# A 64-row expert block's high and low parts stacked on 128 partitions, with its spreads spaced out over two pairs of PSUM banks

## The chip, the cores and the metric

The kernel runs on one core of one Trainium2 chip. The metric is the device time of one execution in microseconds; three runs of the kernel before have a median of 2049.76 us (2049.07 to 2051.22).

## What is computed

The reference is a long chain for 512 tokens of 1024 features: a first transformer block (FFN, two attentions, FFN), a second one with a convolution and an mLSTM, and last a hierarchical mixture of experts. Only this last part is touched. Every token goes to two of 32 experts, each with 512 inner features; in short:

```python
def hierarchical_moe(h, rg_w, rg_b, re_w, re_b, w_gate, w_up, w_down):
    ...
    def expert_block(args):
        xb, e = args
        a = xb @ w_gate[e]
        u = xb @ w_up[e]
        return (jax.nn.silu(a) * u) @ w_down[e]

    ys = lax.map(expert_block, (xs, block_expert)).reshape(n_slots, D)
    ys = ys * slot_gate[:, None].astype(ys.dtype)
    out = jnp.zeros((T, D), ys.dtype).at[slot_tok].add(ys)
```

## The kernel before

The tokens, sorted by expert, are cut into 32 blocks (`SLOTS`), each of which uses one expert's weights. 27 blocks have 64 rows and are called narrow here; five have 128 rows and are called wide: numbers 6, 11, 16, 21 and 26 (`WIDE_AT`, line 47). A block's weights are six loads of 1 MB: four for gate and up, two for down. The loads go through a ring of 13 buffers (`RINGS`, line 48); `e_done` tells the ring that a part has been used, and `e_advance` issues the next load on SyncE's queue, which waits there until the buffer is free.

`moe_blocks` (line 1790) runs over the blocks in a software pipeline. Iteration i (line 1806) does four things on TensorE:

- the gate/up products of block i+1 (`e_gu`): eight chunks c of 128 features, for each a gate and an up product. For a narrow block the stationary operand has 64 columns, and gate and up fill the two halves of one `mm` bank, as two column tiles of the array that run side by side. A wide block takes two `mm` banks and the whole array. Every fp32 product is two records in the trace;
- the turn of block i (`e_turn`): four transposes of the activated rows `eh` into a `tp` bank, which ScalarE copies to `hT`;
- four spreads of block i-1, one for each tile of 128 tokens (`spread`): the block's results are multiplied with a 0/1 matrix `pick` that has a one where a row belongs to a token, into two banks (`po` for the first 512 features, `tp` for the last), and VectorE adds both banks into `x` (`spread_add`);
- the down products of block i (`e_down`): four chunks c, for each two halves of 512 features, into `sc`. For a narrow block these two halves are again the two halves of one bank's partitions: features 0 to 511 on partitions 0 to 63, features 512 to 1023 on 64 to 127.

After that `keep` makes `pick` (VectorE) and splits the results into a high part, rounded to fp32r by ScalarE, and a low part, the rest, by VectorE's subtraction. Both parts of a narrow block stand in one tile `y` of 128 partitions, high in columns 0 to 511 and low in columns 512 to 1023. The product with `pick` runs in fp32r, once with the high part and once with the low, so that the sum is exact enough. A narrow block's spread has four such products: for each part, one with the upper 64 partitions into `po` and one with the lower 64 into `tp`. A wide block's has four too, of 128 partitions each.

The order on TensorE is the order in the code. `e_gu` calls a hook behind each chunk: behind chunk 1 it makes the turn, and behind chunks 3, 5 and 7 one spread each. The fourth spread is left for the loop at line 1822, which runs after `e_gu` and `e_act` and ahead of `e_down`. In iteration 31, which has no gate/up products, all four spreads stand in that loop.

PSUM has eight banks: three `mm`, two `sc`, two `tp` and one `po` (lines 337 to 347). Each is taken in rotation, and a product that takes one waits until its last use has been read.

Of the kernel before, what the change touches and what calls it, by code (L numbers as in the profile page):

```python
# [8 lines left out]
F32 = mybir.dt.float32  # L9
F32R = mybir.dt.float32r  # L10
I32 = mybir.dt.int32
BF16 = mybir.dt.bfloat16
AF = mybir.ActivationFunctionType
# [303 lines left out]
class Kern:  # L317
# [1416 lines left out]
        self.nc.scalar.activation(t[:, 0:4 * m], p[:, 0:4 * m], AF.Copy)  # L1734
        return t

    def e_down(self, i, h, part=None):

        if part is None:
            part = lambda j: self.e_parts[i, 4 + j]  # L1740
        if i is not None and self.wide(i):
            m, ps = 128, (self.sc(), self.sc())
        else:
            p = self.sc()
            m, ps = 64, (p[0:64], p[64:128])
        for c in range(4):
            for f in range(2):
                o = (c % 2) * 1024 + f * 512
                self.nc.tensor.matmul(ps[f], h[:, c * m:(c + 1) * m], part(c // 2)[:, o:o + 512],
                                      start=(c == 0), stop=(c == 3))  # L1750
            if i is not None and c % 2:
                self.e_done(i, 4 + c // 2)
        return (ps[0], ps[1]) if m == 128 else (p,)

    def yt(self, dt=F32):
# [3 lines left out]
    def keep(self, ps, tok):  # L1759
        nc = self.nc  # L1760
        s = self.et("pick", F32R)
        nc.vector.tensor_scalar(s, self.e_iota, tok, None, op0=ALU.is_equal)
        parts = []
        for p in ps:
            y = self.yt(F32R)
            self.split_act(p, y[:, 0:512], y[:, 512:1024])
            parts.append(y)
        return s, parts

    def spread_to(self, kept, t, banks, first=True, last=True):  # L1770

        s, parts = kept
        n = len(parts)
        for i in range(2):
            for f in range(2):
                a = slice(0, 128) if n == 2 else slice(64 * f, 64 * f + 64)
                self.nc.tensor.matmul(banks[f], s[a, t * 128:(t + 1) * 128], parts[f % n][a, 512 * i:512 * i + 512],
                                      start=first and i == 0, stop=last and i == 1)

    def spread_add(self, t, banks):  # L1780
        for f in range(2):
# [1 line left out]
            self.nc.vector.tensor_add(o, o, banks[f].rearrange("p (c d) -> p c d", c=4))  # L1783

    def spread(self, kept, t):
        banks = self.po(), self.tp()
        self.spread_to(kept, t, banks)
        self.spread_add(t, banks)

    def moe_blocks(self):  # L1790
        nc, tc = self.nc, self.tc
        self.e_advance()
        self.e_iota = self.xpool.tile([128, 512], F32, name="e_iota")
        nc.gpsimd.dma_start(self.e_iota, self.I["c_main"][:, 512:1024])
        gr = self.xpool.tile([128, D], F32, name="gains")
        self.rows_in(ROW_FN, D, gr)
        self.g3 = gr.rearrange("p (c d) -> p c d", c=KC)
        rows = lambda i: (self.block_rows(self.first_row(self.ex[i]), 128 if self.wide(i) else 64)
                          if i < SLOTS else None)
        fac = lambda i: [self.fac[:, j, self.ex[i]:self.ex[i] + 1] for j in range(2)]  # L1800
        x = self.block_rows(self.row1, 64)
        self.by_block()
        xn = rows(2)
        h = self.e_act(self.first, fac(0))
        kept = hT = None
        for i in range(SLOTS):
            todo = [lambda t=t, k=kept: self.spread(k, t) for t in range(4)] if kept else []

            def hook(c):
                nonlocal hT  # L1810
                if c == 1:
                    hT = self.e_turn(h)
                elif c % 2 and todo:
                    todo.pop(0)()
            if i + 1 < SLOTS:
                ps = self.e_gu(i + 1, x, hook)
                x, xn = xn, rows(i + 3)
                hn = self.e_act(ps, fac(i + 1))
            else:
                hook(1)  # L1820
                hn = None
            while todo:
                todo.pop(0)()
            ps = self.e_down(i, hT)
            kept = self.keep(ps, self.tok[:, self.ex[i]:self.ex[i] + 1])
            h = hn
        self.final(kept)


        more = nc.values_load(self.wl[0:1, 2 * PLACES:2 * PLACES + 1], min_val=0, max_val=PLACES - SLOTS)  # L1830
        with tc.For_i(0, more, 1) as it:
            e = nc.sync.value_load(self.wl[0:1, ds(it + SLOTS, 1)], min_val=0, max_val=NE - 1)
            x = self.block_rows(self.first_row(it + SLOTS), 64)
            ix = self.xpool.tile([128, 1], F32, name="m_tok", tag="ix", bufs=1)
            fx = self.xpool.tile([128, 2], F32, name="m_fac", tag="fx", bufs=1)
            nc.vector.tensor_copy(ix, self.tok[:, ds(it + SLOTS, 1)])
            for j in range(2):
                nc.vector.tensor_copy(fx[:, j:j + 1], self.fac[:, j, ds(it + SLOTS, 1)])
            parts = []
            for j in range(6):  # L1840
                t = self.e_raw("raw2")
                nc.sync.dma_start(t, self.I["we"][ds(e, 1), j].rearrange("a p f -> (a p) f"))
                parts.append(t)
            p = self.mm()
            ps = p[0:64], p[64:128]
            for c in range(KC):
                s = slice((c % 4) * 512, (c % 4 + 1) * 512)
                for k in range(2):
                    nc.tensor.matmul(ps[k], x[:, c, 0:64], parts[2 * (c // 4) + k][:, s], start=(c == 0), stop=(c == KC - 1))
            h = self.e_act(ps, [fx[:, j:j + 1] for j in range(2)])  # L1850
            kept = self.keep(self.e_down(None, self.e_turn(h), lambda j: parts[4 + j]), ix)
            self.final(kept)
# [65 lines left out]
```

## Time and profile before

| what | us |
|---|---|
| median of three runs | 2049.76 |
| profiled execution | 2049.38 |
| its span | 2047.5 |
| TensorE busy in the span | 1904.2 |
| VectorE busy | 1067.7 |
| ScalarE busy | 620.7 |
| all 32 blocks, first gate/up products to the end | 577.7 |

The span is the time from the first to the last instruction; the execution's own time is 1.9 us longer. Busy times are sums over an engine's instructions; matmuls overlap, so a busy TensorE is not one at its peak. The first gate/up products start at 1469.8 us. All times below are counted from the start of the span. In a timeline a row may stand for several equal instructions (x8), with the start of the first and the time to the end of the last; what stands in brackets is the engine's idle time ahead of it and who ended it. "128*64" is the part of the array in rows and columns that a product uses.

### The profile page before, as it was taken

The page shows a single profiled execution, that of the slowest core. Times are in us where ns is not written, and L with a number is a line of the kernel's source. Part 1 is how long each engine was busy: PE and PEld are TensorE (multiplying, and loading weights), DVE is VectorE, ACT ScalarE, POOL GpSimd, SP SyncE. Part 2 cuts the span into 40 slices and gives each one's busy share as a digit, 9 for nine tenths or more (in the row PEclk, how much of TensorE's full clock was granted, in tenths as well). Part 3 has the DMA queues.
Part 4 walks back from the last instruction along what each step waited for, and adds up shares of the span by engine and source line. Part 5 has one row for each costly group of instructions (what it writes and reads, how often), then busy time and mean ns, then how long its engine had stood idle before and what let it go on. Part 6 is the DMA issues. An engine that isn't in the chain of part 4 may idle for free.

```text
span 2047.5 us, 22693 instructions
## 1 busy us (share of the span) xinstructions
PE 1904.2 (93%) x8588; PEld 1299.9 (63%) x8588; DVE 1067.7 (52%) x1628; ACT 620.7 (30%) x979; POOL 382.2 (19%) x293
## 2 busy tenths in 40 slices
PE   7999999999999999999999878689499999999995
PEld 5888888887777788888888756567233333333331
DVE  6543344425578555443445789985534444444344
ACT  4322223325565343221324234442321111111112
POOL 2000000125554430000002456524100000000001
PEclk9999999999999999999999989799799999999997
DMA  5233222322222122222222211112799999899981
GB/s 174 83 139 144 85 101 103 123 77 80 87 68 82 62 103 98 88 103 103 84 101 103 73 60 41 42 42 86 294 373 421 419 376 391 334 370 360 369 318 42
DMA packets 52443, 337.89 MB, mean 165 GB/s; under 512 B 5868, under 2 KB 8724, under 8 KB 13804
## 3 DMA queue, kind: packets, MB, share of 16 engines
q1 hardware_dynamic: 48972, 326.13, 41.9%
q0 software_dynamic: 3072, 9.24, 1.5%
q8 instruction: 69, 1.13, 0.2%
q10 hardware_dynamic: 288, 1.05, 0.1%
q14 instruction: 42, 0.34, 0.0%
HBM read 332.18 MB, written 8.16 MB: 166 GB/s over the span
## 4 chain that ended last, share of the span: by engine, by line
PE 81%; DVE 12%; DMA 3%; issue 2%; ACT 1%; POOL 1%; SPq 0%; POOLq 0%; DVEq 0%; ACTq 0%
PE mm L302 64%; PE sc L302 8%; PE po L302 6%; DVE conv L302 4%; PE tp L302 3%; DVE qk L302 2%; DVE x L302 1%; DVE score L302 1%; DMA x_rows<-x 1%; DMA eraw<-in_we_dram 1%; DVE att_s L302 1%; DVE rs_t L302 0%; DMA x<-in_xT_dram 0%; DVE rs_y L302 0%; DMA raw<-in_wd_dram 0%
## 5 line engine op out<-in xcount | busy, mean ns | idle before, releaser
L302 PE MATMUL mm<-nhi,whi 128*128 128x512 f32 x1120 | 446.9, 399 | 13.2 <-ACT whi L356 9.4
L302 PE MATMUL mm<-nlo,whi 128*128 128x512 f32 x1120 | 439.2, 392 | 1.2 <-DVE nlo L302 1.2
L302 PE MATMUL mm<-nhi,wlo 128*128 128x512 f32 x1120 | 438.6, 392 | 0.7 <-DVE wlo L302 0.7
L356 ACT ACTIVATE whi<-raw 128x1024 fp32r<-128x1024 f32 x220 | 231.1, 1053 | 306.8 <-PE mm L302 118.2
L302 DVE TENSOR_TENSOR wlo<-raw,whi 128x1024 fp32r<-128x1024 f32 x155 | 198.1, 1279 | 209.8 <-ACT whi L356 209.8
L302 PE MATMUL mm<-eraw,xb 128*64 128x512 f32 (+1 forms) x992 | 274.0, 603 | 0.0
L302 PEld LDWEIGHTS mm<-nhi,whi 128*128 128x128 f32 x1120 | 211.8, 189 | 62.6 <-ACT whi L356 9.4
L302 PEld LDWEIGHTS mm<-nlo,whi 128*128 128x128 f32 x1120 | 211.7, 189 | 46.7 <-DVE nlo L302 4.1
L302 PEld LDWEIGHTS mm<-nhi,wlo 128*128 128x128 f32 x1120 | 211.5, 189 | 46.6 <-DVE wlo L302 1.7
L302 DVE TENSOR_TENSOR x<-x,po 128x512 f32<-128x512 f32 x124 | 85.2, 687 | 219.9 <-PE tp L302 183.6
L302 POOL TENSOR_TENSOR wlo<-raw,whi 128x1024 fp32r<-128x1024 f32 x65 | 163.8, 2525 | 151.2 <-ACT whi L356 140.1
L302 PEld LDWEIGHTS mm<-eraw,xb 128*64 128x64 f32 (+1 forms) x992 | 81.2, 145 | 133.2 <-issue 125.6
L302 PE MATMUL mm<-hhi,whi 128*128 128x512 f32 x352 | 136.9, 389 | 0.0
L302 PE MATMUL mm<-hlo,whi 128*128 128x512 f32 x352 | 136.9, 389 | 0.0
L302 PE MATMUL mm<-hhi,wlo 128*128 128x512 f32 x352 | 136.9, 389 | 0.0
L302 PE MATMUL sc<-eraw,hT 128*64 128x512 f32 (+1 forms) x512 | 136.8, 609 | 0.0
L302 PE MATMUL po<-y,pick 64*128 64x512 f32 (+1 forms) x248 | 94.5, 447 | 25.1 <-DVE x L302 24.5
L302 POOL TENSOR_TENSOR acc<-sq,sq 128x512 f32<-128x512 f32 x6 | 8.7, 1457 | 580.2 <-ACT sq L455 580.2
L302 PEld LDWEIGHTS po<-y,pick 64*128 64x128 f32 (+1 forms) x248 | 38.4, 186 | 112.8 <-DVE x L302 79.3
L302 POOL TENSOR_SCALAR rs_v<-fss 128x1 f32<-128x1 f32 x3 | 0.6, 190 | 542.4 <-ACT eraw L1866 542.2
L302 PEld LDWEIGHTS sc<-eraw,hT 128*64 128x64 f32 (+1 forms) x512 | 44.1, 147 | 77.2 <-issue 75.3
L302 PE MATMUL tp<-y,pick 64*128 64x512 f32 (+1 forms) x248 | 92.5, 439 | 0.0
(447 smaller groups left out, 2566.8 us busy)
## 6 DMA issues: line engine op xcount, KB each, us to landing
eraw<-in_we_dram SPq DMA_DIRECT2D x192, 1024.0 KB, 7.8
raw<-in_wd_dram SPq DMA_DIRECT2D x109, 1024.0 KB, 4.8
bias_rows<-bias_by_distance SPq DMA_DIRECT2D x4, 960.0 KB
bias<-bias_rows POOLq DMA_DIRECT2D x12, 256.0 KB, 3.1
x_rows<-x SPq DMA_DIRECT2D x4, 512.0 KB, 18.4
x<-in_xT_dram SPq DMA_DIRECT2D x3, 512.0 KB, 8.3
raw<-in_wd_dram SPq DMA_DIRECT2D x2, 512.0 KB, 9.0
out_dram<-eraw SPq DMA_DIRECT2D x2, 512.0 KB
```

Of the source, the lines that this page charges most:

```text
L302: return f(*a, **k)
L356: self.nc.scalar.activation(hi, raw, AF.Copy)
```

## The change

- `keep`: a narrow block's two halves are laid out the other way. For the first 512 features the high part stands on partitions 0 to 63 of `y`'s columns 0 to 511 and the low part on partitions 64 to 127 of the same columns; for the other 512 features, in columns 512 to 1023, the high part stands on 64 to 127 and the low part on 0 to 63. It takes two copies on ScalarE and two subtractions on VectorE of 64 partitions each, in place of one each of 128.
- `spread_to`: a narrow block's spread is two products of 128 partitions, one for each bank, in place of four of 64 partitions. `pick` has the same tokens on both halves of its partitions, so that a product adds high and low part itself. A wide block's four products stay; those for `po` now come ahead of those for `tp`.
- `spread`: tiles 1 and 3 take an `mm` bank in place of `po`.
- `moe_blocks` and `e_down`: the turn comes behind chunk 0 of the gate/up products, the spreads of tiles 0 to 2 behind chunks 3, 5 and 7 as before, and that of tile 3 behind chunk 0 of the down products, by a hook that `e_down` calls.

```diff
-    def e_down(self, i, h, part=None):
+    def e_down(self, i, h, part=None, hook=None):
...
             if i is not None and c % 2:
                 self.e_done(i, 4 + c // 2)
+            if hook:
+                hook(c)
         return (ps[0], ps[1]) if m == 128 else (p,)
...
         parts = []
-        for p in ps:
+        if len(ps) == 1:
+
             y = self.yt(F32R)
-            self.split_act(p, y[:, 0:512], y[:, 512:1024])
+            for f in range(2):
+                a, b, c = slice(64 * f, 64 * f + 64), slice(64 - 64 * f, 128 - 64 * f), slice(512 * f, 512 * f + 512)
+                nc.scalar.activation(y[a, c], ps[0][a], AF.Copy)
+                nc.vector.tensor_sub(y[b, c], ps[0][a], y[a, c].bitcast(F32))
             parts.append(y)
+        else:
+            for p in ps:
+                y = self.yt(F32R)
+                self.split_act(p, y[:, 0:512], y[:, 512:1024])
+                parts.append(y)
         return s, parts
...
         s, parts = kept
-        n = len(parts)
-        for i in range(2):
-            for f in range(2):
-                a = slice(0, 128) if n == 2 else slice(64 * f, 64 * f + 64)
-                self.nc.tensor.matmul(banks[f], s[a, t * 128:(t + 1) * 128], parts[f % n][a, 512 * i:512 * i + 512],
-                                      start=first and i == 0, stop=last and i == 1)
+        w = s[:, t * 128:(t + 1) * 128]
+        for f in range(2):
+            y = parts[f:f + 1] if len(parts) == 2 else parts
+            r = [y[0][:, 0:512], y[0][:, 512:1024]] if len(parts) == 2 else [y[0][:, 512 * f:512 * f + 512]]
+            for i, a in enumerate(r):
+                self.nc.tensor.matmul(banks[f], w, a, start=first and i == 0, stop=last and i == len(r) - 1)
...
     def spread(self, kept, t):
-        banks = self.po(), self.tp()
+        banks = self.mm() if t % 2 else self.po(), self.tp()
...
             def hook(c):
                 nonlocal hT
-                if c == 1:
+                if c == 0:
                     hT = self.e_turn(h)
-                elif c % 2 and todo:
+                elif c % 2 and c > 1 and todo:
                     todo.pop(0)()
...
             else:
-                hook(1)
+                hook(0)
                 hn = None
+                while todo:
+                    todo.pop(0)()
+            ps = self.e_down(i, hT, hook=lambda c: c % 2 == 0 and todo and todo.pop(0)())
             while todo:
                 todo.pop(0)()
-            ps = self.e_down(i, hT)
```

On TensorE, the end of iteration 2, whose three blocks are narrow, before: spread 2 (`po` 10848), spread 3 (`po` 10871), and the down products (`sc`).

```order
L302 MATMUL mm_10800<-eraw_10638,xb_10661 64x512
L302 MATMUL mm_10800<-eraw_10648,xb_10661 64x512
L302 MATMUL po_10848<-y_10797,pick_10795 128x512
L302 MATMUL tp_10849<-y_10797,pick_10795 128x512
L302 MATMUL po_10848<-y_10797,pick_10795 128x512
L302 MATMUL tp_10849<-y_10797,pick_10795 128x512
L302 MATMUL po_10871<-y_10797,pick_10795 128x512
L302 MATMUL tp_10872<-y_10797,pick_10795 128x512
L302 MATMUL po_10871<-y_10797,pick_10795 128x512
L302 MATMUL tp_10872<-y_10797,pick_10795 128x512
L302 MATMUL sc_10879<-eraw_10650,hT_10806 64x512 x4
L302 MATMUL sc_10879<-eraw_10672,hT_10806 64x512 x4
```

The same place now:

```order
L302 MATMUL mm_10796<-eraw_10638,xb_10661 64x512
L302 MATMUL mm_10796<-eraw_10648,xb_10661 64x512
L302 MATMUL po_10840<-y_10791,pick_10789 128x512
L302 MATMUL tp_10841<-y_10791,pick_10789 128x512
L302 MATMUL sc_10861<-eraw_10650,hT_10800 64x512 x2
L302 MATMUL mm_10864<-y_10791,pick_10789 128x512
L302 MATMUL tp_10865<-y_10791,pick_10789 128x512
L302 MATMUL sc_10861<-eraw_10650,hT_10800 64x512 x2
L302 MATMUL sc_10861<-eraw_10672,hT_10800 64x512 x4
```

Each spread has two products in place of four, and spread 3 has moved between the first chunk of the down products and the second, into an `mm` bank.

On ScalarE, what follows the down products of iteration 1, before, with the semaphores that are waited for: the copy that makes `y`, the copy of the turn, and the next block's rows (`xb`).

```order
L362 ACTIVATE y_10797<-sc_10765 128x512 [waits PE_49]
L1734 ACTIVATE hT_10806<-tp_10805 128x256 [waits DVE_49,PE_49]
L1691 TENSOR_LOAD work_list_10383
L1691 ISA x2
L1696 ISA
L1696 ACTIVATE xb_10865<-xs 128x8x64 [waits PE_49,Activation_49]
```

The same place now:

```order
L1771 ACTIVATE y_10791<-sc_10753 64x512 [waits PE_49]
L1771 ACTIVATE y_10791<-sc_10753 64x512 [waits DVE_49]
L1734 ACTIVATE hT_10800<-tp_10799 128x256 [waits PE_49]
L1691 TENSOR_LOAD work_list_10383
L1691 ISA x2
L1696 ISA
L1696 ACTIVATE xb_10855<-xs 128x8x64 [waits PE_49,Activation_49]
```

There are two copies of half the height, and the second waits for VectorE, whose first subtraction reads the same bank; the turn's copy stands behind it.

## Rows read from the trace of the kernel before

**Rows 1.** The page, its first line.

```profile
span 2047.5 us, 22693 instructions
```

**Rows 2.** Windows: length, busy time of each engine, clock, DMA share, GB/s.

```profile
1501.40:1650.00 148.60, 141.83 (x620) 49.66 (x617) 64.07 (x101) 22.85 (x38) 0.00 (x0) 1.00 1.01 421
1650.00:1983.00 333.00, 319.16 (x1307) 116.08 (x1305) 134.78 (x213) 48.14 (x81) 0.00 (x0) 1.00 0.94 363
```

**Rows 3.** Waits of TensorE, 1501.4 to 2022: us in total, times, longest.

```profile
PE po L302 <- DVE x L302: 24.5, 33, 0.8
```

**Rows 4.** Timeline of iteration 13, TensorE, ScalarE, VectorE: start, us, work.

```profile
1704.31 1.89 PE L302 MATMUL mm<-eraw,xb 128*64 128x512 f32 x8
...
1704.52 0.60 ACT L362 ACTIVATE y<-sc 128x512 fp32r<-128x512 f32 x1 [5.02 <-PE sc L302]
...
1705.15 0.69 DVE L302 TENSOR_TENSOR y<-sc,y 128x512 fp32r<-128x512 f32 x1 [2.41 <-ACT y L362]
...
1708.38 0.49 PE L302 MATMUL po<-y,pick 64*128 64x512 f32 x1
...
1709.04 1.94 PE L302 MATMUL mm<-eraw,xb 128*64 128x512 f32 x8
...
1710.91 0.49 PE L302 MATMUL po<-y,pick 64*128 64x512 f32 x1
...
1713.44 0.50 PE L302 MATMUL po<-y,pick 64*128 64x512 f32 x1
...
1714.73 0.68 ACT L1724 ACTIVATE eg<-mm,fac 64x512 f32<-64x512 f32 x1
...
1714.95 0.49 PE L302 MATMUL po<-y,pick 64*128 64x512 f32 x1 [0.78 <-DVE x L302]
...
1715.61 3.65 PE L302 MATMUL sc<-eraw,hT 128*64 128x512 f32 x16
...
1719.10 1.89 PE L302 MATMUL mm<-eraw,xb 128*64 128x512 f32 x8
```

**Rows 5.** Timeline of TensorE, iteration 17: spreads 2 and 3 of wide block 16.

```profile
1784.57 0.50 PE L302 MATMUL po<-y,pick 128*128 128x512 f32 x1
...
1786.31 0.50 PE L302 MATMUL po<-y,pick 128*128 128x512 f32 x1 [0.55 <-DVE x L302]
...
1787.45 1.08 PE L302 MATMUL sc<-eraw,hT 128*64 128x512 f32 x4
```

**Rows 6.** Timeline of TensorE in the mLSTM: fp32 products (`qk`), then fp32r ones.

```profile
1321.19 0.60 PE L302 MATMUL po<-qk,qk 128*128 128x256 f32 x2
...
1321.86 0.39 PE L302 MATMUL mm<-nlo,whi 128*128 128x512 f32 x1
1322.09 0.40 PE L302 MATMUL mm<-nhi,wlo 128*128 128x512 f32 x1
```

**Rows 7.** Timeline of TensorE, iteration 15: gate/up products of wide block 16.

```profile
1742.30 3.70 PE L302 MATMUL mm<-eraw,xb 128*128 128x512 f32 x8
1745.93 0.50 PE L302 MATMUL po<-y,pick 64*128 64x512 f32 x1
...
1746.59 0.70 PE L302 MATMUL mm<-eraw,xb 128*128 128x512 f32 x1
```

**Rows 8.** Timeline of TensorE: first turn, block 6's first products, last down products.

```profile
1492.42 0.46 PE L302 MATMUL tp<-cmain,eh 64*128 64x64 f32 x4
...
1560.75 1.55 PE L302 MATMUL mm<-eraw,xb 128*128 128x512 f32 x3
...
2015.68 6.21 PE L302 MATMUL sc<-eraw,hT 128*64 128x512 f32 x16
```

**Rows 9.** Tile `eraw`, the 36th load (block 6): issue, time to landing.

```profile
L1670 SPq DMA_DIRECT2D eraw<-in_we_dram x1: 333/333/333, 1536.7 to 1536.7; - x1
...
DMA to landing us min/median/max: 19.8/19.8/19.8
```

**Rows 10.** Timeline of weight loads among dense fp32r products.

```profile
897.26 0.19 PEld L302 LDWEIGHTS mm<-nlo,whi 128*128 128x128 f32 x1
```

## The prediction

> **What bounds the kernel now.** I first read the page for the span, 2047.5 us [rows 1], and then the windows over the expert blocks, where the change lies. From 1501 to 1983 us TensorE is busy for 141.8 of 148.6 us and then for 319.2 of 333 us, its clock granted in full [rows 2]. The loads run at 421 GB/s in the first stretch and at 363 GB/s in the second: there the queues are fed as buffers come free, and not the reverse. The waits of TensorE's products in this stage name one releaser that counts, the adds into `x` on VectorE: 24.5 us in 33 waits [rows 3]; no product waits for a load. The timeline of one iteration shows where: spreads 0, 1 and 2 stand alone between gate/up products, but spread 3 follows spread 2 directly and stands idle for 0.78 us, because there is one `po` bank and VectorE has to add it first [rows 4]. So TensorE's row of instructions is the path, and what leaves it comes off the end, as long as the loads keep up.
>
> **What a spread costs, two ways.** In [rows 4] a narrow spread takes 0.66 us from its first product to the next gate/up product (1708.38 to 1709.04). Its four products are two pairs of 64-row tiles; po and tp start together, so a pair costs one stream. The stacked form has two products on all 128 rows, one after the other: again two streams. The nearest row for it is a wide block's spread: four 128-row products in 1.14 us (1786.31 to 1787.45) [rows 5], 0.23 us each by the step of such products in [rows 6] plus 0.22 for entering and leaving; two would take 0.68. Between narrow products I therefore put the stacking at nothing, though it halves the instructions. Its bounds there are 0.2 us less (two streams of 0.23 and no change-over) and 0.19 us more (a weight load that shows, below).
>
> A change-over has a price of its own. Sixteen down records take 3.49 us [rows 4], 0.43 for each pair once the change-over in front is taken off; eight gate/up records between two spreads take 1.87 us (1709.04 to 1710.91), 0.15 more than four times 0.43. Beside wide gate/up products (128 rows by 128 columns, one record at a time) today's 64-row pairs are another array shape: eight records and a spread take 4.29 us (1742.30 to 1746.59), of which 3.44 are records at 0.43 [rows 7]. The stacked spread has the shape of its neighbours there. What such a neighbour costs can be seen where an fp32 product goes over to an fp32r one in another bank, both 128 by 128: from the first of two 256-column records to the second fp32r product it is 0.67 us [rows 6]; two times 0.21 and one 0.23 make 0.65, so next to nothing is lost. A stacked spread among wide products should cost 0.46 us and the cycle 3.90: 0.39 less.
>
> **The sum over iterations 1 to 30**, which have both gate/up products and spreads (wide blocks are 6, 11, 16, 21 and 26):
> - All three blocks narrow, 15 iterations. Now 2.17 us from spread 2 to the down products (1713.44 to 1715.61) [rows 4]. After: spread 2, 0.66, and spread 3 behind the first chunk of the down products, 0.66 and one more change-over, 0.15. 2.17 - 1.47 = 0.70; times 15: 10.5.
> - Wide gate/up products, 5 iterations. The 0.70; 0.39 each for spreads 0 and 1; about 0.20 for spread 2, which saves the way in only, since narrow down products follow. 1.68 times 5: 8.4.
> - Wide down products, 5 iterations. The 0.70; spread 3 among wide down products costs 0.46 and not 0.81, 0.35 less; spread 2's way out, 0.15. 1.20 times 5: 6.0.
> - Spreads of a wide block, 5 iterations. Their products stay as they are. Now 2.88 us from spread 2 to the down products (1784.57 to 1787.45) [rows 5]; after, 1.14 and 1.14 + 0.15: 0.45 less, times 5: 2.3.
>
> Together 27.2 us. At its new place the wait is covered: spread 3 takes a `mm` bank and the tp of spread 1, both added long before, some 1.6 us after spread 2 started.
>
> **Smaller terms.** The turn moves from behind chunk 1 to behind chunk 0. In iteration 0 it waits for block 0's `eh` until 1492.42 [rows 8], so chunk 1 now comes after that wait: 0.9 us lost, once. Keeping a narrow block becomes a chain of four half-height pieces (ScalarE, VectorE, ScalarE, VectorE; the order shows ScalarE's second one waiting for VectorE). Half the height is not half the time: 0.68 us for `eg` with 64x512 on ScalarE beside 0.60 for `y` with 128x512 [rows 4]. So the chain is 2 x (0.60 + 0.69) plus gaps, 2.7 us, where it was 1.3. It starts 0.2 us into the gate/up products and spread 0 comes 4.07 us into them [rows 4], so 1.2 us are left over; behind ScalarE's second wait stand hT's copy, needed only at the down products, and `xb` of a later block. In the last iteration the spreads follow each other directly; three waits of 0.78 us fall away, since two pairs of banks let TensorE run ahead, and the chain's 1.3 us come in: 1.0 us gained. After the last block the chain lies open: its second ScalarE piece with the gaps, while VectorE waits, is about 0.75 us. The last down products run at half clock now (6.21 us where 3.65 is usual) [rows 4, 8], behind the sparse spreads before them. These stay about as sparse, so I leave that; if the clock held, 2.6 us more would go.
>
> Sum: 27.2 - 0.9 + 1.0 - 0.75 = 26.6 us. From the profiled execution, 2049.38 us, that gives 2022.8; it lies 0.4 us below the median of the runs shown, which I neglect.
>
> **Do the loads keep up?** A block is 6.29 MB; at 421 GB/s that is 14.94 us, and a narrow iteration will take 14.1. The stock is thinnest at the start. The load for block 6 that is issued at 1536.7 lands 19.8 us later [rows 9], at 1556.5, for products that start at 1560.75 [rows 8]: 4.2 us in hand. Four iterations will have gained 2.8 by then and iteration 0 lost 0.9, so 2.3 remain, and then a wide block takes longer than its loads. Later, five iterations with one wide block need 31.5 MB in some 82 us, 384 GB/s, about a tenth below what the queues have shown. Were the stock at the start gone, the narrow iterations of the first 60 us would go at 14.94 us and lose 3 us in all.
>
> **Rivals.**
> 1. The array empties between fp32 products and an fp32r spread although the shape is the same. For it: the row without loss has 256 columns and goes in one direction only. Against: that row. Then wide neighbours gain the 0.70 and no more, 27.2 falls by 4.9 + 2.5, and the time is 2030.
> 2. The weight load of the second stacked product shows. One of 128x128 takes 0.19 us [rows 10]. If it can't run under a product that uses all rows, 80 spreads beside narrow products lose 0.19 each (15.2 us) and 20 beside wide ones 0.38 (7.6): 26.6 - 22.8 leaves 4, time 2045. Against: products with such a load each step at 0.23 us [rows 6, 10], so the load lies under the stream before. The Trainium skill has such a rule (TensorE: Matmul & The Clock Gate, "The mechanism" in Part 3): a weight load overlaps running products only where their row groups differ, which those of the pairs do and those of the stacked products don't. The rows speak against it here.
> 3. Slower: the four-piece chain. Its VectorE pieces write the other 64 partitions than they read. If the pieces took twice their time, the chain would be 5.3 us and spread 0 would stand for 1.4 us in each of 25 iterations with narrow spreads, 35 us against 27 gained: 2058. Gain turns to loss where the pieces take about 1.8 times as long. Against: `eg` in [rows 4] shifts partitions already (from 0 to 63 to 64 to 127) and takes 0.68.
> 4. It doesn't do what it says, or is hidden: spread 3 still waits for an add, so that only the change-over is new, or the loads can't go beyond the 363 GB/s of now. Then 2045 to 2050. Against: the bank numbers in the order, and the 421 GB/s in [rows 2].
>
> **How the numbers follow.** Forecast 0.68, rival 1 0.15, rival 2 0.05, rival 3 0.05, rival 4 0.07. The range runs from the forecast with the clock held and the stacking's lower bound taken in part (2017) to rival 1 with some waits for loads (2032). Faster by over 0.2%, which is about what a measurement of this kernel can tell from no change: the forecast, rival 1 and part of rivals 2 and 4, 0.88; within it 0.06; slower 0.06.
>
> **What would show it.** In the timeline after: no idle time before spread 3; 0.66 us for a stacked spread among narrow products and 0.46 among wide ones, with eight wide records and a spread at 3.90; an iteration of three narrow blocks at 14.1 us instead of 14.79 (1704.31 to 1719.10); spread 0 starting without a wait for `y`; the loads at some 380 GB/s in the second stretch. The prediction is wrong if TensorE's products wait for `eraw` or `po` waits for `y`, or if the first wide record still starts 0.33 us after the second stacked product.

## The result and the profile after

The changed kernel takes 2019.18 us in the median (2014.62 to 2021.5), the kernel before 2050.49 (2049.07 to 2051.78) on the same chip: a ratio of 0.9845, 95% interval 0.9833 to 0.9857. The profiled execution took 2021.5 us. Its page begins with:

```profile
span 2019.7 us, 22160 instructions
...
PE 1896.2 (94%) x8372; PEld 1300.5 (64%) x8372; DVE 1086.4 (54%) x1655; ACT 636.5 (32%) x1006; POOL 382.3 (19%) x293
```

The span is 27.8 us shorter than in [rows 1]. TensorE has 216 products fewer, but the busy time fell by only 8 us; most of what went was idle. The windows of the expert blocks (length, busy time of each engine, clock, DMA share, GB/s) answer to [rows 2]:

```profile
1501.40:1650.00 148.60, 148.60 (x583) 52.81 (x580) 71.59 (x113) 28.96 (x49) 0.00 (x0) 1.00 1.01 421
1650.00:1960.00 310.00, 310.00 (x1175) 114.83 (x1175) 145.42 (x229) 56.58 (x95) 0.00 (x0) 1.00 0.98 394
```

TensorE never stands still there, and the loads run at 394 GB/s in the second stretch where they ran at 363. The waits of TensorE from 1501.4 to 2022 us (line waited for, us in total, times, longest) answer to [rows 3]. None of them starts before 1984 us, that is, all lie in the last iteration and behind the last block:

```profile
PE mm L302 <- DVE y L302: 2.3, 2, 1.5
PE mm L302 <- DVE x L302: 2.1, 2, 1.1
PE po L302 <- DVE y L302: 1.1, 1, 1.1
PE tp L302 <- DVE y L302: 0.9, 1, 0.9
```

The timeline of iteration 13, the one of [rows 4]; TensorE's rows first, then the chain that makes `y` on ScalarE and VectorE:

```profile
1695.40 1.03 PE L302 MATMUL mm<-eraw,xb 128*64 128x512 f32 x4
1696.36 0.46 PE L302 MATMUL tp<-cmain,eh 64*128 64x64 f32 x4
1696.75 2.80 PE L302 MATMUL mm<-eraw,xb 128*64 128x512 f32 x12
1699.48 0.50 PE L302 MATMUL po<-y,pick 128*128 128x512 f32 x1
1699.82 0.39 PE L302 MATMUL tp<-y,pick 128*128 128x512 f32 x1
1700.14 1.94 PE L302 MATMUL mm<-eraw,xb 128*64 128x512 f32 x8
...
1705.20 1.08 PE L302 MATMUL sc<-eraw,hT 128*64 128x512 f32 x4
1706.21 0.50 PE L302 MATMUL mm<-y,pick 128*128 128x512 f32 x1
1706.55 0.40 PE L302 MATMUL tp<-y,pick 128*128 128x512 f32 x1
1706.87 2.80 PE L302 MATMUL sc<-eraw,hT 128*64 128x512 f32 x12
1709.50 0.60 PE L302 MATMUL mm<-eraw,xb 128*64 128x512 f32 x2
...
1695.62 0.59 ACT L1771 ACTIVATE y<-sc 64x512 fp32r<-64x512 f32 x1 [4.55 <-PE sc L302]
1696.96 0.59 ACT L1771 ACTIVATE y<-sc 64x512 fp32r<-64x512 f32 x1 [0.75 <-DVE y L302]
...
1697.58 0.69 DVE L302 TENSOR_TENSOR y<-sc,y 64x512 fp32r<-64x512 f32 x1 [0.66 <-ACT y L1771]
```

The iteration takes 14.10 us (1695.40 to 1709.50) where it took 14.79. Spread 3 (1706.21) has no idle time in brackets. A stacked spread takes 0.66 us (1699.48 to 1700.14), exactly what four 64-row products took. The chain ends at 1698.27, 1.2 us before spread 0.

Wide gate/up products (iteration 15, answering to [rows 7]):

```profile
1730.85 0.79 PE L302 MATMUL po<-y,pick 128*128 128x512 f32 x1
1731.26 0.19 PEld L302 LDWEIGHTS tp<-y,pick 128*128 128x128 f32 x1 [0.24 <-issue]
1731.48 0.39 PE L302 MATMUL tp<-y,pick 128*128 128x512 f32 x1
...
1731.71 3.59 PE L302 MATMUL mm<-eraw,xb 128*128 128x512 f32 x8
1734.74 0.79 PE L302 MATMUL mm<-y,pick 128*128 128x512 f32 x1
```

From one spread to the next is 3.89 us (1730.85 to 1734.74) where it was 4.29; the first product behind the spread follows 0.23 us after the last spread product.

### Where the time went, by kind of iteration

The table is worked out from the starts of TensorE's products: an iteration runs from its first gate/up product to the next one's. It has the kernels that differ in the middle of the stage. "Narrow" is the usual one of 14 iterations (a few are 0.1 us longer), the three kinds with a wide block have five each.

| us | before | after | spaced only | stacked only | chain twice | two groups |
|---|---|---|---|---|---|---|
| narrow | 14.79 | 14.10 | 14.10 | 14.57 | 15.47 | 13.39 |
| wide gate/up | 21.90 | 20.18 | 21.20 | 20.66 | 20.18 | 19.85 |
| wide down | 18.57 | 17.32 | 17.92 | 18.14 | 18.50 | 16.98 |
| spreads of a wide block | 16.48 | 16.00 | 16.01 | 16.23 | 16.01 | 15.27 |
| iterations 1 to 29 | 492.34 | 465.36 | 473.52 | 479.60 | 490.51 | 449.06 |
| iteration 0 | 11.11 | 11.97 | 11.96 | 11.11 | 11.97 | 11.11 |
| start of iteration 30 to the last down products | 21.90 | 20.40 | 19.48 | 22.28 | 24.65 | 19.35 |
| last down products to the end | 31.83 | 30.34 | 29.30 | 32.00 | 33.42 | 30.17 |

From before to after: 26.98 us off iterations 1 to 29, 1.50 off iterations 30 and 31, 1.49 off the part behind them, 0.86 more in iteration 0. That is 29.1. The remaining 1.3 us are lost ahead of block 1's gate/up products, where the code is the same; in the twelve profiled executions that stand behind this text, block 1's products start anywhere from 1488.67 to 1493.71 us.

### The profile page after: what moved, and what is told of

Its sections match the earlier page's. It is cut to its first block, busy times and chain, and to the rows that moved or that the text cites. A ratio compares the mean times of both kernels' runs of the same rounds, so it can differ in the third digit from the quotient of the medians.

```text
span 2019.7 us, 22160 instructions
## 1 busy us (share of the span) xinstructions
PE 1896.2 (94%) x8372; PEld 1300.5 (64%) x8372; DVE 1086.4 (54%) x1655; ACT 636.5 (32%) x1006; POOL 382.3 (19%) x293
## 3 DMA queue, kind: packets, MB, share of 16 engines
q10 hardware_dynamic: 288, 1.05, 0.1%
## 4 chain that ended last, share of the span: by engine, by line
PE 80%; DVE 13%; DMA 3%; issue 2%; ACT 1%; POOL 1%; SPq 0%; POOLq 0%; DVEq 0%; ACTq 0%
PE mm L302 65%; PE sc L302 8%; PE tp L302 4%; DVE conv L302 4%; PE po L302 3%; DVE qk L302 2%; DVE score L302 1%; DMA x_rows<-x 1%; DVE x L302 1%; DMA eraw<-in_we_dram 1%; DVE rs_t L302 1%; DVE att_s L302 1%; DVE hm L302 0%; DVE nlo L302 0%; DMA x<-in_xT_dram 0%
## 5 line engine op out<-in xcount | busy, mean ns | idle before, releaser
L302 DVE TENSOR_TENSOR x<-x,po 128x512 f32<-128x512 f32 x62 | 42.7, 688 | 125.3 <-PE po L302 125.3
L1696 ACT ACTIVATE xb<-xs 128x512 f32 (+1 forms) x31 | 21.9, 706 | 233.4 <-PE mm L302 233.2
L302 DVE TENSOR_TENSOR up<-mm,row 128x512 f32<-128x512 f32 x44 | 30.4, 691 | 110.5 <-PE mm L302 110.5
L302 DVE SCALAR_TENSOR_TENSOR conv<-ca,vecs,conv 128x502 f32<-128x502 f32 (+18 forms) x78 | 88.1, 1185 | 0.2
L302 DVE TENSOR_TENSOR y<-sc,y 64x512 fp32r<-64x512 f32 (+1 forms) x64 | 44.1, 689 | 80.7 <-ACT y L1771 62.2
```

What stands on the lines that cost most here:

```text
L302: return f(*a, **k)
L1696: self.nc.scalar.activation(x[:, :, 0:m], self.xs[:, :, ds(row, m)], AF.Copy)
```

## The experiments

The theory is that of the prediction: TensorE's row is the path, spacing removes the wait for VectorE's adds, stacking gains only where the neighbours use the whole array, and the loads and the chain keep up. The rivals are those of the prediction, and that one half of the change does all the work.

### The changed kernel once more

The same kernel, to see what varies.

> The changed kernel once more, for its time beside the others and for a second trace. Its first four runs lay between 2014.6 and 2021.5 us. Theory (the expert blocks take the same time in every run, what varies lies in the routing stage ahead of them and in the half-clock stretches around the last block): the iterations 1 to 30 take 465.36 us again within 0.3 us (1503.62 to 1968.98 in the first trace), and the difference of the spans stands before or behind them. Rival (waits for loads within the blocks): the iterations differ by microseconds.

2020.69 us (2019.84 to 2022.47), ratio 0.9854 (0.9838 to 0.9871). Iterations 1 to 29 took 465.36 us, the same to the hundredth. From block 0's first gate/up products to block 2's it took 32.90 us in place of 33.34, and the clock fell at another place (last section). So between these two executions iterations 1 to 29 repeat, and what differs lies ahead of them and behind them.

### Spacing without stacking

The changed kernel with `keep` and `spread_to` of before: full-height pieces, four 64-row products to a spread.

```diff
-        if len(ps) == 1:
-            y = self.yt(F32R)
-            for f in range(2):
-                ...
-        else:
-            for p in ps:
-                ...
+        for p in ps:
+            y = self.yt(F32R)
+            self.split_act(p, y[:, 0:512], y[:, 512:1024])
+            parts.append(y)
```

> The new spacing (turn behind chunk 0, spread 3 behind the first chunk of the down products, mm bank for tiles 1 and 3) with the old layout of y and four 64-row products for each narrow spread. Theory (the spacing takes the 0.78 us waits away and costs one change-over of 0.15 us; the layout counts beside wide products only): 0.70 us less in 15 all-narrow iterations, about 0.70 in the 10 with a wide neighbour, 0.45 in 5 with a wide block's spreads, 0.9 lost once, 2.3 gained in the last iteration, since the longer chain is absent: about 21 us less than before, 2029. In its trace no idle time before spread 3, a narrow spread at 0.66 us, the cycle of eight wide records and a spread still at 4.29 us. Rival (the gain comes from halving the products): about the time of before.

2026.92 us (2022.83 to 2029.75), ratio 0.9876 (0.9859 to 0.9892). The narrow iteration takes 14.10 us, as with stacking: among narrow products stacking gains nothing, and all of the 0.70 us is the spacing's. The wide ones are 1.02 (gate/up) and 0.60 us (down) longer than after. Its timeline of TensorE among wide gate/up products shows why:

```profile
1737.33 3.70 PE L302 MATMUL mm<-eraw,xb 128*128 128x512 f32 x8
1740.96 0.50 PE L302 MATMUL mm<-y,pick 64*128 64x512 f32 x1
...
1741.62 3.70 PE L302 MATMUL mm<-eraw,xb 128*128 128x512 f32 x8
```

The cycle is still 4.29 us (1737.33 to 1741.62), though there is no wait in it: the 0.4 us that stacking takes off is the price of the other array shape. Stacking is worth 5 x 1.02 + 5 x 0.60 = 8.1 us here, and costs something at the end: the last two rows of the table are 0.9 and 1.0 us shorter without it, since the chain of half-height pieces lies open there. Of the 0.9 us 0.34 are the clock, though: the repeat of the changed kernel, at full clock in that place, takes 20.06 us where the table has 20.40.

### Stacking without spacing

The kernel before with `keep` and `spread_to` of after; the order and the banks stay as before.

```diff
-        parts = []
-        for p in ps:
+        if len(ps) == 1:
+            y = self.yt(F32R)
+            for f in range(2):
+                ...
```

> The stacked layout and two products for a narrow spread, with the order, hooks and banks of before: spread 3 follows spread 2 in the one po bank. Theory: nothing among narrow products; 0.98 us in each of 5 iterations with wide gate/up products (0.39, 0.39, 0.20), 0.15 in 5 with wide down products; the wait before spread 3 shrinks by about 0.22 us in 25 iterations, since po is complete after the first of two products and not after the third of four; 1.3 us lost in the last iterations to the longer chain: about 10 us less than before, 2040. If the wait does not shrink: 4 us less, 2046. Rival (halving the products is worth a quarter of a microsecond for every narrow spread): 25 us less.

2037.42 us (2036.66 to 2038.08), ratio 0.9934 (0.9917 to 0.995). Spread 3 still waits, but for less time than in [rows 4]; TensorE's waits to 1990 us:

```profile
PE po L302 <- DVE x L302: 14.7, 29, 0.5
```

and spreads 2 and 3 in its timeline:

```profile
1708.41 0.50 PE L302 MATMUL po<-y,pick 128*128 128x512 f32 x1
1708.75 0.40 PE L302 MATMUL tp<-y,pick 128*128 128x512 f32 x1
1709.69 0.50 PE L302 MATMUL po<-y,pick 128*128 128x512 f32 x1 [0.55 <-DVE x L302]
```

0.55 us where it was 0.78: `po` now needs one product, which comes first, so its add can start a product's time sooner (0.23 us). This holds for wide blocks too, since their products were put in order by bank. The two halves of the change alone take 18.8 and 12.7 us off iterations 1 to 29, but both at once 27.0 and not 31.6. By the table 5.4 us are counted twice, the part of the wait that either half removes (0.22 or 0.23 in 24 iterations); 0.17 in each of the five with wide down products go the other way, since there spread 3 profits from its new shape only at its new place.

### One bank for `po` in the new places

```diff
-        banks = self.mm() if t % 2 else self.po(), self.tp()
+        banks = self.po(), self.tp()
```

> The changed kernel with po for all four tiles instead of an mm bank for tiles 1 and 3. Theory (the place of spread 3 removes the wait and not the second pair of banks: VectorE has added spread 2's po 1.2 us after its start, spread 3 comes 1.66 us after it): the 30 iterations as in the changed kernel, and waits only in the last one, where the spreads follow each other: 0 to 2 us over the changed kernel. Rival (the banks are what removes the wait): 0.5 us and more in each of 30 iterations, 15 us and more over the changed kernel.

2021.99 us (2020.96 to 2023.82), ratio 0.986 (0.9843 to 0.9876); iterations 1 to 29 take 465.36 us once more, without a wait. At the new distances the second pair of banks does nothing there. It works in the last iteration, where the spreads follow each other: 11.70 us from iteration 30's down products to the last ones, against 10.60 after. TensorE's waits have a line more than after, all of it in that iteration:

```profile
PE po L302 <- DVE x L302: 1.3, 3, 0.6
```

What takes off the 0.78 us is the place behind the first chunk of the down products alone.

### The turn behind chunk 1 again

```diff
-                if c == 0:
+                if c == 1:
...
-                hook(0)
+                hook(1)
```

> The changed kernel with the turn put back behind chunk 1. If moving the turn costs what the prediction says, iteration 0 (first gate/up products of block 1 to those of block 2) falls from 11.97 to 11.11 us and no other iteration changes by more than 0.05 us; spread 0 then stands directly behind no turn in either case. If the place of the turn matters beyond iteration 0 (a late `hT`), the narrow iterations leave 14.10 us.

2017.91 us in one run. Iteration 0 takes 11.11 us, as expected; but iteration 1 takes 14.65 where 14.10 was expected. Of the 0.86 us about 0.55 came back: block 2's products now start at 1499.78, before their second load has landed (1500.06), and chunk 4 at 1504.88 before the fourth (1505.03). In the timeline of weight loads (what stands in brackets is the idle time and who ended it):

```profile
1500.10 0.25 PEld L302 LDWEIGHTS mm<-eraw,xb 128*64 128x64 f32 x3 [0.18 <-DMA eraw<-in_we_dram]
```

The second load, issued at 1490.83, took longer to land than usual:

```profile
DMA to landing us min/median/max: 9.2/9.2/9.2
```

In the six other traces with the turn behind chunk 1 (the kernel before, stacking without spacing, and the four with two groups below) it took 7.8 to 8.6 us and landed 0.4 to 1.1 us ahead of block 2's products, and iteration 1 has its usual length in each. So the loss in iteration 0 is real, and that most of it comes back is shown for this one execution only.

### Each piece of the chain twice

The changed kernel, with each half-height copy and subtraction issued twice. This puts a price on rival 3.

```diff
-                nc.scalar.activation(y[a, c], ps[0][a], AF.Copy)
-                nc.vector.tensor_sub(y[b, c], ps[0][a], y[a, c].bitcast(F32))
+                for _ in range(2):
+                    nc.scalar.activation(y[a, c], ps[0][a], AF.Copy)
+                for _ in range(2):
+                    nc.vector.tensor_sub(y[b, c], ps[0][a], y[a, c].bitcast(F32))
```

> The changed kernel, with each of the four half-height pieces of a narrow block's chain (ScalarE, VectorE, ScalarE, VectorE) issued twice, so that the chain takes about 5.3 us in place of 2.65. This prices rival 3. In the changed kernel's trace the chain ends 1.2 us before spread 0. If that slack is real, spread 0's second product (`tp`) waits about 1.3 us in each of the 25 iterations that spread a narrow block, and the time rises by 26 to 35 us there and by some 4 us in the last iteration and behind the last block: 2046 to 2058. Rival: the pieces overlap or the slack is larger than it looks; then TensorE shows no wait and the time stays within 5 us of 2020.

2052.8 us (2050.51 to 2056.14), ratio 1.0015 (1.0005 to 1.0026): the whole gain is gone. TensorE's waits from 1505 to 2000 us:

```profile
PE tp L302 <- DVE y L302: 21.7, 20, 1.1
```

and one of them in the timeline:

```profile
1997.93 0.50 PE L302 MATMUL po<-y,pick 128*128 128x512 f32 x1
1999.57 0.47 PE L302 MATMUL tp<-y,pick 128*128 128x512 f32 x1 [1.14 <-DVE y L302]
```

The slack of 1.2 us is real, and the mechanism of rival 3 too: 1.37 us in a narrow iteration. But it bites in 20 iterations, not in 25. Where the gate/up products are wide, the four chunks ahead of spread 0 take some 7 us, which covers even the doubled chain (20.18 us in both kernels). So the price was 26.5 us in iterations 1 to 30 and 6 behind them.

### Spreads in two groups

The changed kernel with the turn behind chunk 1, spreads 0 and 1 together behind chunk 3 and spreads 2 and 3 together behind chunk 7. A second spread directly behind the first waited 0.55 us with one `po` bank (stacking without spacing), so the two pairs of banks should be of use now.

```diff
-                if c == 0:
+                if c == 1:
                     hT = self.e_turn(h)
-                elif c % 2 and c > 1 and todo:
+                elif c in (3, 7) and todo:
+                    todo.pop(0)()
                     todo.pop(0)()
...
-                hook(0)
+                hook(1)
```

> The changed kernel with the turn behind chunk 1 and the four spreads in two groups: 0 and 1 together behind chunk 3 of the gate/up products, 2 and 3 together behind chunk 7. With two pairs of banks a second spread needs no wait, and each group saves one change-over. By the stacked spread's 0.66 us alone against 0.46 us without a change-over, and the 0.15 us behind it, a group should save 0.35 us: narrow iterations 14.10 to 13.41 us, 0.35 less where the gate/up or the down products are wide, 0.70 less for a wide block's spreads, 0.86 less in iteration 0. That is 18 us; the loads then have 1.9 us of stock fewer than needed at block 6, so about 2 us come back as waits for `eraw`: 2003 to 2005. Rival: change-overs cost nothing, or the second spread waits for VectorE's adds; then 2019 to 2021, or more with the waits visible.

2002.25 us (2000.52 to 2004.67), ratio 0.9776 (0.9759 to 0.9792). Its timeline of TensorE in a narrow iteration:

```profile
1689.54 0.50 PE L302 MATMUL po<-y,pick 128*128 128x512 f32 x1
1689.88 0.39 PE L302 MATMUL tp<-y,pick 128*128 128x512 f32 x1
1690.11 0.39 PE L302 MATMUL mm<-y,pick 128*128 128x512 f32 x1
1690.34 0.40 PE L302 MATMUL tp<-y,pick 128*128 128x512 f32 x1
1690.67 3.65 PE L302 MATMUL mm<-eraw,xb 128*64 128x512 f32 x16
1694.25 0.50 PE L302 MATMUL po<-y,pick 128*128 128x512 f32 x1
...
1695.37 3.65 PE L302 MATMUL sc<-eraw,hT 128*64 128x512 f32 x16
```

Two spreads take 1.13 us, not 2 x 0.66, and sixteen gate/up records 3.58, not 2 x 1.87: 0.35 us for each group, as expected from the price of a change-over. The narrow iteration is at 13.39 us (13.41 expected). Spread 3 follows spread 2 directly again, but with a second bank it does not wait: the pair takes 1.12 us to the down products (1694.25 to 1695.37) where the kernel before needed 2.17 [rows 4]. That is 1.05 us less; the new places alone took off 0.70, since there spread 3 pays a change-over of its own. So the second bank, at the old places, should have been worth more than the spacing; this is worked out from these rows, and no run has the bank alone.

The loads kept up better than feared. TensorE has only one wait from 1501.4 to 1958 us, at block 6:

```profile
PE mm L302 <- DMA eraw<-in_we_dram: 0.3, 1, 0.3
```

That iteration takes 20.36 us in place of 19.85, 0.5 us and not 2. The later window shows the queues at 415 GB/s, next to the 421 of [rows 2]: by that there is little left to gain here before the loads bound the stage.

```profile
1650.00:1945.00 295.00, 295.00 (x1170) 117.39 (x1167) 142.43 (x227) 55.89 (x95) 0.00 (x0) 1.00 1.01 415
```

### Two groups, and the last two blocks in the old layout

```diff
-        if len(ps) == 1:
+        if len(ps) == 1 and stack:
...
-            kept = self.keep(ps, self.tok[:, self.ex[i]:self.ex[i] + 1])
+            kept = self.keep(ps, self.tok[:, self.ex[i]:self.ex[i] + 1], i < SLOTS - 2)
```

> The kernel with spreads in two groups, and the last two blocks kept in the old layout (full-height pieces, four 64-row products to a spread), since there the chain lies open. Down products of iteration 30 to those of iteration 31: 9.7 us in place of 10.3 to 10.6. From the last down products to the end: 29.3 in place of 30.4 us. Together 1.5 to 2 us below the kernel with two groups alone. Rival: the stacked layout's shorter adds make up for it; then the two are equal within 0.5 us.

2001.5 us (2000 to 2002.95), ratio 0.9766 (0.9749 to 0.9782): 0.75 us below two groups alone where 1.5 to 2 were expected, and not told apart from it by these runs. In its trace the last iteration was shorter by 0.58 us (8.86 against 9.44, down products to down products), but the last down products ran partly at half clock (5.35 us for 3.65), which hid the rest. So both were run once more.

> The kernel with spreads in two groups, once more, beside the next one. Iterations 1 to 29 take 449.06 us again within 0.6 (a load wait more or less at block 6); the median stands between 2000.5 and 2004.7.

> The kernel with two groups and the last two blocks in the old layout, once more. By the first pair's traces the last iteration is 0.58 us shorter and the part behind the last down products 0.89 us shorter when the clock is taken out (30.98 us against 30.17, with the sixteen down records at 5.35 us in place of 3.65). If the clock falls in both kernels about as often, its median is 1.0 to 1.5 us below the other's. Rival: the shorter last part leaves TensorE at half clock more often and the two medians are equal within 0.5 us.

Two groups: 2003.72 us (2001.51 to 2005.91), ratio 0.9774 (0.9759 to 0.9788). With the old layout at the end: 2001.41 (1997.63 to 2002.06), ratio 0.9759 (0.9745 to 0.9773). Over both pairs of runs, nine of each, the medians are 2003.72 and 2001.41. The traces of the second pair show full clock in both last down products, and 30.14 us against 29.27 from there to the end, and 9.99 against 8.87 ahead of it. The difference behind the last down products is the layout's alone; in the one ahead of them the clock had fallen among the spreads of the kernel with two groups only. The intervals still overlap, so a gain of 1 to 2 us is likely rather than shown. The changed kernel's eight runs have a median of 2020.15 us, so the two versions beat it by 16 and 19 us.

## Why the prediction was right

The forecast was 2022.8 us in a range of 2017 to 2032; measured were 2019.18 us. Faster was forecast, by the mechanism that the traces show. By its steps:

- **What bounds the kernel.** Right: what left TensorE's row came off the end, and no wait took its place until the last iteration.
- **The sum over iterations 1 to 30.** 0.70 us for a narrow iteration (0.70 forecast), 1.72 where gate/up is wide (1.68), 1.25 where down is wide (1.20), 0.48 for a wide block's spreads (0.45). With 15, 5, 5 and 5 of them 27.7 us, forecast 27.2.
- **Stacking among narrow products, put at nothing.** Right: 0.66 us either way, and 14.10 us with and without it. The forecast's lower bound, 0.2 us less, can't be had by a spread alone.
- **The turn.** 0.86 us lost in iteration 0 (0.9 forecast). Undone, most of it came back in the one execution of that kernel, as a wait for a slow load of block 2; the other traces with the turn behind chunk 1 have no such wait.
- **The last iteration.** 0.79 us gained in the profiled execution and 1.13 in the repeat (1.0 forecast); the two differ because the clock fell in one. That they fit is in part luck. In the kernel before, the clock had fallen during its last spread, which took 1.15 us to the down products (2015.68 in [rows 8]) where 0.66 is usual:

```profile
2014.53 0.79 PE L302 MATMUL po<-y,pick 64*128 64x512 f32 x1 [0.78 <-DVE x L302]
```

0.49 us of the gain are this. With the clock at full on both sides the gain is 0.64 us, so the term was mis-sized. The chain's new cost is there as described: the waits for `y` rise from 0.60 us (0.37 and 0.23) to 2.02 (1.08 and 0.94), 1.4 more where 1.3 was forecast. But of the three waits for adds one is left in part, for `tp`, which the change gives no further bank; in the repeat:

```profile
1987.72 0.50 PE L302 MATMUL tp<-y,pick 128*128 128x512 f32 x1 [0.46 <-DVE x L302]
```

- **The open chain behind the last block.** Mis-sized: 1.1 us, not 0.75. The forecast counted ScalarE's second piece alone; VectorE's second stands in the open as well. In the timeline after, ScalarE's first copy and TensorE's first two starts behind the last down products:

```profile
1993.14 0.59 ACT L1771 ACTIVATE y<-sc 64x512 fp32r<-64x512 f32 x1 [7.45 <-PE sc L302]
...
1994.51 0.49 PE L302 MATMUL mm<-y,pick 128*128 128x512 f32 x1 [1.47 <-DVE y L302]
...
1995.86 2.37 PE L302 MATMUL mm<-y,pick 128*128 128x512 f32 x4 [0.86 <-DVE y L302]
```

and before:

```profile
2022.00 0.60 ACT L362 ACTIVATE y<-sc 128x512 fp32r<-128x512 f32 x1 [12.27 <-PE sc L302]
...
2023.37 0.73 PE L302 MATMUL mm<-y,pick 64*128 64x512 f32 x3 [0.23 <-DVE y L302]
```

From the copy to the product that needs the last piece it is 2.72 us where it was 1.37; of the 1.35 more, 1.07 reach the end.
- **The clock in the last down products, left alone.** In the profiled execution it held (3.65 us where [rows 8] has 6.21), so 2.6 us more went. It was named as the lower end of the range; the repeat held too. It isn't a sure gain: in the ten executions of this change and its variants with a single chain, these products took 3.65 us seven times and 4.57, 5.35 and 5.61 in the others.
- **The loads.** They kept up. The load for block 6, issued at 1538.3, landed 19.9 us later, 1.9 us ahead of its products at 1560.10 (2.3 forecast).
- **Rival 1** (an empty array between fp32 and fp32r) fell: 3.89 us for the cycle, 3.90 forecast without that loss. **Rival 2** (a weight load that shows) fell as well: among wide products `tp`'s 128x128 load runs from 1731.26 to 1731.45, and its product starts at 1731.48, the next one 0.23 us later; in a group of two spreads the products with such loads step by 0.23 us. So for products that use all rows the trace speaks against the rule of the Trainium skill (TensorE: Matmul & The Clock Gate, "The mechanism" in Part 3) that the prediction cited for it: a load was hidden though its product shares its rows with the running one. (The same section excepts loads for a background weight buffer; no run here tells whether that is what hid this one.) **Rival 3** did not come, but its price was real when the chain was made twice as long; its count of iterations was wrong (20, not 25). **Rival 4** fell: no wait is left in iterations 1 to 30, and the loads reached 394 GB/s, and 415 in the version with two groups.

The median is 3.6 us below the forecast. The profiled execution, at 2021.5 us, is 1.3 below it: 2.6 by the clock and 0.5 by the iterations, less 0.2 in the last iteration, 0.3 behind the last block and 1.3 ahead of block 1. The median lies another 2.3 us lower. Which part of the program was shorter in those runs no trace shows, so that stays open. That the number fits so well is in part luck: two terms that the forecast left out, 2.6 us of clock and 1.3 ahead of block 1, went opposite ways.

## What to carry to other kernels

A wait for one bank's drain goes away by other work between two uses or by a second bank. Price both. Here other work took off 0.70 us, because the product that moved pays for a change-over at its new place, and by the rows of the kernel with two groups a second bank takes off some 1.05. Where the uses already stand apart, a second bank adds nothing (one bank for `po`). Products with another array shape than their neighbours pay a change-over, 0.35 us here beside streams of 0.46 for a spread: give them the shape of their neighbours, or, if they can't have it, put them in groups, which was worth another 16.3 us in iterations 1 to 29, beside the 27.0 of the change. And a change that lengthens a chain off the path should be priced by its slack (1.2 us here) and by the places where there is none, the last iteration and the end.

## What the runs showed of the hardware

The clock at the end is not a property of the program. In the profiled execution it was at half (1.2 GHz) for 3.41 us among the last spreads, after the turn and the waits for the chain; in the repeat of the same kernel it stayed at full (2.4 GHz) in the same place, and fell first behind the last down products. The windows of the two executions (columns as above; the repeat runs some 1 us ahead) show it. The first profile of the changed kernel:

```profile
1985.64:1989.05 3.41, 2.89 (x7) 1.93 (x7) 3.15 (x6) 0.06 (x1) 0.00 (x0) 0.50 0.00 0
```

The repeat:

```profile
1985.64:1989.05 3.41, 2.86 (x11) 1.14 (x11) 3.41 (x7) 0.00 (x0) 0.00 (x0) 1.00 0.00 0
```

At half clock the spreads took 0.43 us a product instead of 0.23. A difference of up to 2.6 us between two kernels that comes from a few products at the end is therefore not evidence on its own; that between iterations in mid-stage is good to 0.02 us.

The price of a change-over goes by the group of products and not by the product. A group of two (0.66 us) and one of four (1.13 us) both took 0.20 us beyond their streams of 0.23 each, and 0.15 in the products behind them. Full-height fp32r products among 64-column pairs pay it as 64-row pairs do there: 0.66 us for either kind of spread.
